# A two-layer diffusion backbone on one Trainium2 core: gated unit ahead of layer 1's first queries, block work between up and down, a reordered layer step

## The chip, the cores and the metric

The kernel runs on 1 core of one Trainium2 chip. Its time is the device time of one execution, in microseconds (us). The kernel before takes 1481.97 us, the median of 3 runs (1481.2 to 1482.17). One execution, taken with the hardware profiler, took 1484.51 us.

The core has five engines with a queue of instructions each: PE (TensorE, matrix products; PEld are its weight loads), DVE (VectorE), ACT (ScalarE), POOL (GpSimd) and SP (SyncE, which here only issues DMAs). 16 DMA engines carry data between HBM and the on-chip memory.

## The reference

256 latent tokens and 256 context tokens of width 1024 pass through two layers that share their weights between both streams. Everything is float32.

```python
for i in range(DEPTH):                                  # 2
    with_ctx_out = i < DEPTH - 1                        # layer 1: latents alone come out
    sh1, sc1, g1, sh2, sc2, g2 = split(silu(c) @ w_mod[i] + b_mod[i], 6)     # and csh1.. of c_ctx
    hl = modulate(rms_norm(x,  norm1_g[i]), sh1, sc1)
    hc = modulate(rms_norm(xc, norm1_g[i]), csh1, csc1)
    lat_mix, ctx_mix = token_mixers(hl, hc, ...)        # one projection w_in, three head groups:
        # A: global attention, 6 query heads on 2 key heads, q/k norm and rotary
        # B: gated unit u = a * sigmoid(g), depthwise convolution of 31 taps, layer norm, silu
        # C: window attention (+-128 tokens), 6 heads on 2, with a learned sink per head
    x = x + g1 * (lat_mix @ w_out[i])
    hl = modulate(rms_norm(x, norm2_g[i]), sh2, sc2)
    # the same for xc in layer 0
    y = hierarchical_moe(...)   # top 1 of 4 groups, top 2 of its 8 experts; 32 experts, each
                                # (silu(h @ w_gate[e]) * (h @ w_up[e])) @ w_down[e], 1024 -> 512 -> 1024
    x = x + g2 * y
return rms_norm(x, final_g)
```

## The kernel before, in words

Tokens lie in tiles of 128. Layer 0 works on four tiles (two latent, two context), layer 1 on two for all but keys and values. A float32 matrix product is split in a high and a low part (wh and wl of a weight, hH and hL of an activation), made by a cast on ACT and a difference on DVE or POOL, and taken as three products.

A layer runs in this order. **Modulation**: `mod_load` brings 4 MB of w_mod (tile wm) and returns `compute`, which makes 64 products `pm`. In layer 0 two groups of it stand at the start of the program; the others are put as fills between later products (list `todo`). **Norm and modulation of the tokens**: `rstd` and `modulate` give hT (high) and hL (low). **Projections**: `product_kv` (keys and values, pkv), `gated_unit` (pu), `first_queries` (A) and `project_q(1)` (C), whose steps for one k carry a number of convolution taps (`conv(cv[n][k])`) and of query and key steps (`st`); the tables `cv` and `st` of the configuration say how many. `query_tile` makes the tile tq, which PE then transposes (pqt). **Attention units**: S = q k, its maximum mx, P, its transposes pT, PT and po, for a pair of heads and a token tile; 12 units in layer 1. **Convolution's norm**, **output projection** (`load_wo`, pwo), **router**.

**Experts.** 32 experts go in 16 pairs, two pairs to a quad. `pair` makes gate and up (pgu: 16 products for each, weights in tile we, on half of the array, 64 columns), the product of silu and up (act), its transposes (pat), and down (py). A pair takes 12 weight loads of 1 MB from SP through a ring of eight slots. Four times in a pair `burst(i)` is called: after gate (0), after up (1), after the transposes (2), and in the middle of down (3). The list `at` says what stands in each: the gathers of the next quad's tokens (`mine`: a one-hot step, weights, gathers 0 to 7, written pg), and the eight `adders` of the pair before (two products pc and two DVE instructions each), which add its result to the tokens. pg, pat and pc use the array's whole width.

After layer 0's last pair, `finish` calls the last adders, squares the result (sq) and sums the squares over the tokens with products by ones (ss): layer 1's first norm.

What sets the order: engines PE, DVE and ACT are written out in order by `manual_schedule` in these stretches, SP throughout; else a scheduler places instructions. A record of the trace is not always one instruction: one float32 product appears as two.

Of the names in the rows, rope, gqk, rb, sinkb are small inputs (rotary table, norm gains, router bias, sinks); negsink is -sinkb, which C's softmax uses; wr are the router's weights.

## Time and profile before

| | |
|---|---|
| Time, median of 3 runs | 1481.97 us (1481.2 to 1482.17) |
| Profiled execution | 1484.51 us, of it the span 1482.9 us |
| PE busy | 1410.0 us, 95% |
| DVE busy | 612.1 us, 41% |
| ACT busy | 394.6 us, 27% |
| POOL busy | 85.9 us, 6% |
| DMA | 481.86 MB, mean 325 GB/s |

Layer 0's projections and attention lie before 300 us, its experts from about 313 to 803 us, layer 1's projections and attention to about 962, its router to 1006, its experts to the end. A share of busy time is a mean over stages with different limits; each stage is read for itself. The granted clock is 1.00 at 2.4 GHz and 0.50 at 1.2 GHz; a number between is a mean over a stretch with both.

### The profile page before, as it was taken

What the parts mean: (1) busy time and instruction counts of PE and PEld (TensorE: products, weight loads), DVE (VectorE), ACT (ScalarE), POOL (GpSimd) and SP (SyncE); (2) the same over time, 40 slices, a digit from 0 to 9 for tenths busy, and PEclk for the clock granted to TensorE, in tenths of its full rate; (3) what the DMA queues carried; (4) which work ended last, traced back from release to release, by engine and by line L of the source; (5) the groups of instructions that cost most, each with busy time, mean ns of one, the idle gap of its engine ahead of it and who ended that gap; (6) DMA issues with size and microseconds to landing.
All of it is one profiled execution on the core that took longest, in us unless ns stands there. A gap on an engine that the chain in (4) does not pass through costs nothing. (4 is left out here: it accounts for less than half of the span.)

```text
span 1482.9 us, 20526 instructions
## 1 busy us (share of the span) xinstructions
PE 1410.0 (95%) x8080; PEld 775.2 (52%) x8080; DVE 612.1 (41%) x1379; ACT 394.6 (27%) x954; POOL 85.9 (6%) x146
## 2 busy tenths in 40 slices
PE   6999899999999999998999998989999999999997
PEld 4777677754444544444435776774443343333432
DVE  3469884353223333333334568853222222222223
ACT  3454575430111111100102555652111111110102
POOL 3212000100000000000001020010000000000000
PEclk8999999999999999999999899999999999999999
DMA  9847502399799999999999583087999999999996
GB/s 312 315 156 260 138 2 103 153 359 371 319 402 411 415 409 407 417 408 397 390 401 383 203 292 89 4 361 290 371 419 422 420 421 422 421 420 421 420 418 257
DMA packets 92324, 481.86 MB, mean 325 GB/s; under 512 B 8884, under 2 KB 17296, under 8 KB 47040
## 3 DMA queue, kind: packets, MB, share of 16 engines
q1 hardware_dynamic: 90960, 478.19, 81.3%
q0 software_dynamic: 800, 1.20, 0.4%
q8 instruction: 66, 1.08, 0.3%
q10 hardware_dynamic: 464, 1.11, 0.2%
q14 instruction: 34, 0.28, 0.0%
HBM read 479.42 MB, written 1.05 MB: 324 GB/s over the span
## 5 line engine op out<-in xcount | busy, mean ns | idle before, releaser
L1340 PE MATMUL pgu<-we,xg 128*64 128x512 f32 x1904 | 450.8, 598 | 23.4 <-DMA we<-in_w_gate_dram 13.1
L1340 PEld LDWEIGHTS pgu<-we,xg 128*64 128x64 f32 x1904 | 143.5, 137 | 308.8 <-issue 251.6
L1394 PE MATMUL py<-we,actT 128*64 128x512 f32 x888 | 205.8, 597 | 0.7 <-ACT actT L1355 0.7
L1236 DVE SCALAR_TENSOR_TENSOR xT<-pc,mod,xT 128x256 f32<-128x256 f32 x256 | 104.8, 476 | 177.4 <-PE pc L1233 177.4
L1394 PEld LDWEIGHTS py<-we,actT 128*64 128x64 f32 x888 | 61.9, 136 | 114.8 <-issue 110.8
L1290 ACT COPY xg<-pg 128x256 f32<-128x256 f32 x112 | 36.3, 376 | 309.8 <-PE pg L1286 309.8
L1349 DVE SCALAR_TENSOR_TENSOR act<-pgu,ws,sil 128x512 f32<-128x512 f32 x32 | 24.0, 751 | 194.0 <-PE pgu L1340 185.1
L1244 DVE TENSOR_TENSOR xo<-xo,pc 128x512 f32<-128x512 f32 x62 | 39.8, 683 | 111.3 <-PE pc L1243 111.3
L1285 PE MATMUL pg<-OH,hH 128*128 128x256 f32 x336 | 84.2, 290 | 0.0
L1286 PE MATMUL pg<-OH,hL 128*128 128x256 f32 x336 | 81.7, 283 | 0.0
L634 DVE SCALAR_TENSOR_TENSOR ca<-gpad,cw,ca 128x512 f32<-128x512 f32 (+1 forms) x120 | 73.3, 611 | 0.9
L1285 PEld LDWEIGHTS pg<-OH,hH 128*128 128x128 f32 x336 | 64.2, 191 | 11.4 <-issue 10.5
L281 PE MATMUL pm<-wm,scT 128*32 128x256 f32 (+1 forms) x896 | 64.3, 370 | 2.2 <-DMA wm<-in_w_mod_dram 2.0
L1286 PEld LDWEIGHTS pg<-OH,hL 128*128 128x128 f32 x336 | 64.3, 191 | 0.0
L1344 ACT ACTIVATE sil<-pgu 128x512 f32<-128x512 f32 x32 | 19.2, 598 | 167.1 <-PE pgu L1340 167.1
L1259 DVE TENSOR_TENSOR Yg<-py,g2r 128x512 f32<-128x512 f32 x31 | 21.3, 688 | 100.8 <-PE py L1394 96.5
L1363 POOL CAST se<-ident 32x128 fp32r<-32x128 f32 x32 | 9.1, 286 | 900.8 <-PE pb L1364 871.0
L1261 ACT CAST YH<-py 128x512 fp32r<-128x512 f32 x32 | 18.7, 586 | 151.3 <-PE py L1394 134.4
L1261 ACT CAST YH<-Yg 128x512 fp32r<-128x512 f32 x31 | 19.1, 618 | 141.2 <-DVE Yg L1259 141.2
L1232 PE MATMUL pc<-oht,YH 128*128 128x512 f32 x128 | 55.2, 432 | 0.2 <-ACT YH L1261 0.2
L1233 PE MATMUL pc<-oht,YL 128*128 128x512 f32 x128 | 50.6, 395 | 0.2 <-DVE YL L1262 0.2
L1262 DVE TENSOR_TENSOR YL<-py,YH 128x512 fp32r<-128x512 f32 x32 | 22.1, 691 | 61.2 <-ACT YH L1261 61.2
(434 smaller groups left out, 2125.4 us busy)
## 6 DMA issues: line engine op xcount, KB each, us to landing
we<-in_w_up_dram SPq DMA_DIRECT2D x112, 1024.0 KB, 8.9
we<-in_w_down_dram SPq DMA_DIRECT2D x111, 1024.0 KB, 11.2
we<-in_w_gate_dram SPq DMA_DIRECT2D x110, 1024.0 KB, 11.8
wm<-in_w_mod_dram SPq DMA_DIRECT2D x44, 1024.0 KB, 11.0
wp<-in_w_gate_dram SPq DMA_DIRECT2D x8, 1024.0 KB, 11.2
wp<-in_w_up_dram SPq DMA_DIRECT2D x8, 1024.0 KB, 10.3
we<-in_w_gate_dram SPq DMA_DIRECT2D x16, 512.0 KB, 11.0
we<-in_w_up_dram SPq DMA_DIRECT2D x16, 512.0 KB, 10.2
```

The source lines that it names most:

```text
L281: pe.matmul(p[0][32 * q:32 * q + 32], scT[:, kq, :], ws[128 * kq // nr][:, kq % (nr // 128), c:c + n], start=k == 0, stop=k == KC * nq // ...
L634: ve.scalar_tensor_tensor(a, g, wt, a, op0=OP.mult, op1=OP.add)
L1232: pe.matmul(pc, YH[:, 128 * o:128 * o + 128], oht, start=True, stop=False)
L1233: pe.matmul(pc, YL[:, 128 * o:128 * o + 128], oht, start=False, stop=True)
L1236: ve.scalar_tensor_tensor(xT[:, o, sl], pc[:, sl], mod[l][:, 5, o, s:s + 1], xT[:, o, sl], op0=OP.mult, op1=OP.add)
L1244: ve.tensor_tensor(xo[t][:, sl], xo[t][:, sl], pc, op=OP.add)
L1261: sc.copy(YH[:rows, sl], py)
L1285: pe.matmul(dst, hH[t][:, 128 * k:128 * k + 128], rhs, start=t == 0, stop=False)
L1286: pe.matmul(dst, hL[t][:, 128 * k:128 * k + 128], rhs, start=False, stop=t == NT - 1)
L1290: sc.copy(xg[e][:, k - 1:k + 1, :], v[:, :, e])
L1340: pe.matmul(p[64 * e:64 * e + 64, m, :], xg[:, k, 64 * e:64 * e + 64], w_[e](k % 4), start=k == 0, stop=k == KC - 1)
L1394: pe.matmul(py[64 * e:64 * e + 64, h], actT[:, 128 * f + 64 * e:128 * f + 64 * e + 64], wd[e](f % 2)[:, 512 * h:512 * h + 512], start=f == ...
```

## The change

Six edits, told by place.

1. *Start of the program.* The rotary table and ten small broadcast loads go from POOL's queue, ahead of the weights, to SP's queue (`small_inputs`), behind the first four groups of weights. The router's weights wr go from POOL's queue at the start of a layer to SP's, just ahead of `load_wo`. Of the dummy products of PE, 20 behind the first modulation group become 4, and 12 stand behind the second.
2. *Between the layers.* `compute` is cut in `products` and the rest, so that `finish` can place parts of layer 1's modulation group (m = 2) between the sums; the squares are added up on POOL and DVE to three tiles rather than five; eight dummies and the casts of the key and value weights stand ahead.
3. *Layer 1.* The gated unit comes ahead of the first queries; taps are 2 per k in `first_queries` and 3 per k in `project_q(1)`, before 4 per k in the latter alone.
4. *Attention units* take two consecutive heads (2j and 2j + 1), before heads j and 3 + j; `load_wo` so loads 128 rows at a time, before pieces of 64.
5. *Pairs of layer 0 that gather for a next quad* (13 of 16): nothing but the one-hot step stands between gate and up, nothing in the middle of down; all else stands between up and down, ahead of and behind the transposes.
6. SP issues layer 1's weights in the order in which they are now used.

```diff
@@ -191,23 +191,23 @@
     rope_t = per.tile([128, 2, 2, 64], F32, name="rope")
-    gp.dma_start(rope_t, rope)
-    def bcast_load(t, src, n):
-        gp.dma_start(t, bass.AP(tensor=src.tensor, offset=src.offset, ap=[[0, 128], [1, n]]))
     gqk = per.tile([128, DEPTH, 2, 64], F32, name="gqk")
...
     sinkb = per.tile([128, DEPTH, 6], F32, name="sinkb")
-    for l in range(DEPTH):
-        bcast_load(gqk[:, l, 0, :], qg_d[l], 64)
-        bcast_load(gqk[:, l, 1, :], kg_d[l], 64)
-        bcast_load(rb[:, l, 0:4], bgrp_d[l], 4)
-        bcast_load(rb[:, l, 4:36], bexp_d[l], 32)
-        bcast_load(sinkb[:, l, :], sink_d[l], 6)
     negsink = per.tile([128, DEPTH, 3, 2], F32, name="negsink")
-    gp.tensor_scalar(negsink, sinkb.rearrange("p l (h j) -> p l j h", h=2), -1.0, None, op0=OP.mult)
+    def bcast_load(t, src, n, eng=gp):
+        eng.dma_start(t, bass.AP(tensor=src.tensor, offset=src.offset, ap=[[0, 128], [1, n]]))
+    def small_inputs():
+        sp.dma_start(rope_t, rope)
+        for l in range(DEPTH):
+            bcast_load(gqk[:, l, 0, :], qg_d[l], 64, sp)
+            bcast_load(gqk[:, l, 1, :], kg_d[l], 64, sp)
+            bcast_load(rb[:, l, 0:4], bgrp_d[l], 4, sp)
+            bcast_load(rb[:, l, 4:36], bexp_d[l], 32, sp)
+            bcast_load(sinkb[:, l, :], sink_d[l], 6, sp)
+        gp.tensor_scalar(negsink, sinkb.rearrange("p l (j h) -> p l j h", h=2), -1.0, None, op0=OP.mult)
@@ -270,16 +270,20 @@
-        def compute(two=False, eng=gp, between=None, p=None):
+        def products(ks=range(KC * nq // 4), two=False, p=None):
             if p is None:
...
                 p = p[:, 0:n], p[:, n:n + 16]
-            for k in range(KC * nq // 4):
+            for k in ks:
                 for q in range(4):
...
                               start=k == 0, stop=k == KC * nq // 4 - 1)
+            return p
+        def compute(two=False, eng=gp, between=None, p=None, made=None):
+            p = made or products(two=two, p=p)
             s = K2("ms", (128, n), tag="m")
...
@@ -462,15 +467,9 @@
-        r1 = rstd(ssq0 if l == 0 else ss1[0], 4, D, "n1")
-        if l > 0:
-            finish_mods(l, 1)
         w = win_d[l]
...
         gp.memset(wr[:, :, 36:], 0.0)
-        gp.dma_start(wr[:, :, 0:4], wgrp_d[l].rearrange("(k p) g -> p k g", p=128))
-        gp.dma_start(wr[:, :, 4:36], wexp_d[l].rearrange("(k p) g -> p k g", p=128))
-        h_mul, h_scale, h_shift, hH, hL = modulate(l, r1)
@@ -492,16 +491,19 @@
         first = []
-        if l > 0:
-            early = mod_load(*todo.pop(0), 0, 8)
         for j in range(4):
...
                 load_u(j)
+        if l == 0:
+            small_inputs()
         wKV = lambda k: wkv[k // 4][:, k % 4, :]
         wU = lambda k: wu[k // 2][:, k % 2, :]
+        if l > 0:
+            ws = Splits(wKV, 512)
+        h_mul, h_scale, h_shift, hH, hL = modulate(l, rstd(ss1[0] if l else ssq0, 4, D, "n1"))
@@ -534,12 +536,15 @@
         if l > 0:
+            early[0].products(range(5, 8), p=early[1])
+            pw_ = P1("warm")
+            for _ in range(8):
+                pe.matmul(pw_[:, 0:256], identb, masks.rearrange("p a b -> p (a b)"), start=True, stop=True)
             h_mul(0)
             h_scale(0)
-            ws = Splits(wKV, 512)
             trans.close()
             with tc.high_priority(offset=-cfg["fpri"]):
-                early(True)
+                early[0](made=early[1])
         dve_order = ExitStack()
@@ -550,7 +555,9 @@
         cf = cfg["fill"][l]
-        cv = cfg["cv"][l]
+        cv = cfg["cv"][0] if l == 0 else ((0,) * KC, (2,) * KC, (3,) * KC)
+        st = cfg["st"][0] if l == 0 else ((0, 1, 0, 1, 0, 0, 1, 0), (0, 1, 0, 0, 1, 0, 0, 0), (0, 1, 0, 1, 1, 0, 0, 0))
@@ -578,12 +585,16 @@
+            def dummies(n):
+                for _ in range(n):
+                    pe.matmul(pm[:, 1, 256:512], identb, masks.rearrange("p a b -> p (a b)"), start=True, stop=True)
             modulation(0)
             mul_to(3)
-            for _ in range(20):
-                pe.matmul(pm[:, 1, 256:512], identb, masks.rearrange("p a b -> p (a b)"), start=True, stop=True)
+            dummies(4)
             modulation(1)
+            dummies(12)
             splits(0)
...
@@ -760,7 +771,7 @@
         todo_steps += [key_rstd] + [lambda i=i: key_tile(i, phase[0] == 2) for i in range(4)]
-        for f in (gated_unit, first_queries) if cfg["u1"][l] else (first_queries, gated_unit):
+        for f in (gated_unit, first_queries):
             f()
@@ -799,15 +810,16 @@
             nb = 1 if i < 2 else 2
...
                 for h in range(2):
-                    q = qT[g](3 * h + j, 128 * (i + b))
+                    q, kv = qT[g](2 * j + h, 128 * (i + b)), (2 * j + h) // 3
                     masked = g == 1 and i < 2
                     o, ks = (S[:, h, :], slice(0, 512)) if i < 2 else (S[:, h, 256 * b:256 * b + 256], slice(256, 512))
-                    pe.matmul(o, q, kH[g][:, h, ks], start=True, stop=False)
-                    pe.matmul(o, q, kL[g][:, h, ks], start=False, stop=not masked)
+                    pe.matmul(o, q, kH[g][:, kv, ks], start=True, stop=False)
+                    pe.matmul(o, q, kL[g][:, kv, ks], start=False, stop=not masked)
                     if masked:
...
@@ -923,12 +936,13 @@
             t = [slot("wo").rearrange("p (c f) -> p c f", f=1024) for _ in range(4)]
-            for n, part in enumerate((((0, 0, 2),), ((0, 128, 1), (1, 640, 1)), ((0, 704, 2),))):
-                for h in range(2):
-                    for i, r, m in part:
-                        r += 192 * h
-                        sp.dma_start(t[n][64 * h:64 * h + 64, i:i + m, :], src[r:r + 64 * m].rearrange("(j d) f -> d j f", d=64))
-            sp.dma_start(t[3], src[384:640].rearrange("(c p) f -> p c f", p=128))
+            for n in range(4):
+                c0, c1 = order[2 * n:2 * n + 2]
+                if c1 == c0 + 1:
+                    sp.dma_start(t[n], src[128 * c0:128 * c0 + 256].rearrange("(c p) f -> p c f", p=128))
+                else:
+                    for i, c in enumerate((c0, c1)):
+                        sp.dma_start(t[n][:, i], src[128 * c:128 * c + 128])
             at = {c: (i // 2, i % 2) for i, c in enumerate(order)}
@@ -963,6 +977,8 @@
+        sp.dma_start(wr[:, :, 0:4], wgrp_d[l].rearrange("(k p) g -> p k g", p=128))
+        sp.dma_start(wr[:, :, 4:36], wexp_d[l].rearrange("(k p) g -> p k g", p=128))
         wo = load_wo()
@@ -1537,13 +1553,20 @@
                     q = sq_[o] = square(o, N)
-                    if o in (1, 2, 3):
+                    if o in (1, 2, 3, 4):
                         gp.tensor_tensor(sq_[0], sq_[0], q, op=OP.add)
+                    if o == 6:
+                        ve.tensor_tensor(q, sq_[5], q, op=OP.add)
                 if h == 1:
+                    f = mod_load(*todo.pop(0), 0, 8)
+                    made = f.products(range(2), two=True)
                     p = P1("ss1")
-                    for i, o in enumerate((0, 4, 5, 6, 7)):
-                        sum_tokens(p, sq_[o], NT, i == 0, i == 4)
+                    for i, o in enumerate((0, 7, 6)):
+                        sum_tokens(p, sq_[o], NT, i == 0, i == 2)
+                    f.products(range(2, 5), p=made)
                     ss1.append(p[:, :NT])
+                    early.extend((f, made))
                 return
@@ -1587,10 +1610,18 @@
                     hot = 1 if len(mine) > 4 else 0
-                    at = [adders[:3] + mine[:hot] if qd or e else [weights], mine[hot:6], adders[3:5], adders[5:]]
-                    at[3] += mine[6:]
-                    if not mine:
-                        at[1], at[2] = at[2], []
+                    if mine and not last:
+                        g = mine[hot:]
+                        head, g = (g[:1], g[1:]) if hot else ([], g)
+                        a_ = adders
+                        at = [mine[:hot], head + a_[:2] + g[:2] + a_[2:4],
+                              a_[4:5] + g[2:4] + a_[5:6] + g[4:6] + a_[6:7] + g[6:] + a_[7:], []]
+                    else:
+                        at = [adders[:3] + mine[:hot] if qd or e else [weights], mine[hot:6], adders[3:5], adders[5:]]
+                        at[3] += mine[6:]
+                        if not mine:
+                            at[1], at[2] = at[2], []
                     if qd == 0 and e == 0:
```

On PE, at the end of layer 0's last pair: the last adder (pc), the sums (ss), modulation (pm), the norm's broadcast (rb) and layer 1's first key and value products (pkv). Before:

```order
L1233 MATMUL pc<-oht,YL 128x512
L418 MATMUL ss_6622<-ones,sq 128x1 x4
L281 MATMUL pm<-wm,scT 32x256 x8
L418 MATMUL ss_6622<-ones,sq 128x1 x12
L281 MATMUL pm<-wm,scT 32x256 x3
L418 MATMUL ss_6622<-ones,sq 128x1 x4
L281 MATMUL pm<-wm,scT 32x256 x13
L339 MATMUL rb<-ident,n1r 128x128 x4
L291 MATMUL pm<-ident,ms 128x8 x2
L558 MATMUL pkv<-wh,hT 128x512 x4
```

Now (the pair of weight load and dummy `warm` stands eight times):

```order
L1249 MATMUL pc<-oht,YL 128x512
L281 MATMUL pm<-wm,scT 32x256 x8
L423 MATMUL ss_6633<-ones,sq 128x1 x12
L281 MATMUL pm<-wm,scT 32x256 x12
L344 MATMUL rb<-ident,n1r 128x128 x4
L281 MATMUL pm<-wm,scT 32x256 x12
L542 LDWEIGHTS identb
L542 MATMUL warm<-masks,identb 128x256
...
L565 MATMUL pkv<-wh,hT 128x512 x2
L295 MATMUL pm<-ident,ms 128x8 x2
```

All pm of this group now stand behind the adders, twelve of them behind the broadcast, and the sums are one run of 12 rather than 20 in three runs.

On PE, in a pair of layer 0's experts that gathers, from the transposes (pat) through down (py) to the next pair's gate (pgu); pb is a broadcast that the gather needs. Before:

```order
L1353 MATMUL pat<-ident,act 128x128 x4
L1232 MATMUL pc<-oht,YH 128x512
L1233 MATMUL pc<-oht,YL 128x512
L1232 MATMUL pc<-oht,YH 128x512
...
L1364 MATMUL pb<-posT,se 128x512
L1394 MATMUL py<-we,actT 64x512 x8
L1232 MATMUL pc<-oht,YH 128x512
L1233 MATMUL pc<-oht,YL 128x512
...
L1394 MATMUL py<-we,actT 64x512 x8
L1340 MATMUL pgu<-we,xg 64x512 x16
L1232 MATMUL pc<-oht,YH 128x512
```

Now, from the last gather on:

```order
L1248 MATMUL pc<-oht,YH 128x512
L1249 MATMUL pc<-oht,YL 128x512
L1380 MATMUL pb<-posT,se 128x512
L1410 MATMUL py<-we,actT 64x512 x16
L1356 MATMUL pgu<-we,xg 64x512 x32
L1248 MATMUL pc<-oht,YH 128x512
L1249 MATMUL pc<-oht,YL 128x512
```

The adders inside down are gone to the stretch ahead of it, and so are those behind gate: the next pgu is gate and up in one run.

On DVE, in layer 1, around the first query tiles (tq, of A's queries) and the convolution's taps (ca). Before, tq stand ahead of the first tap:

```order
L438 TENSOR_TENSOR t_7452<-qn,rope 128x12x16 x2
L722 TENSOR_TENSOR tq<-qn,tq 128x4x64
L722 TENSOR_TENSOR tq<-qn,tq 128x2x64
L439 TENSOR_TENSOR qn<-t_7451,t_7452 128x384
L722 TENSOR_TENSOR tq<-qn,tq 128x4x64
L722 TENSOR_TENSOR tq<-qn,tq 128x2x64
L517 TENSOR_TENSOR gpad<-pu,sg 128x256
L632 TENSOR_SCALAR ca<-gpad,cw,vb 128x256
L634 SCALAR_TENSOR_TENSOR ca<-gpad,cw,ca 128x256 x2
```

Now 46 taps stand ahead of the same tq:

```order
L438 TENSOR_TENSOR t_7633<-qn,rope 128x384
L443 TENSOR_TENSOR t_7634<-qn,rope 128x12x16 x2
L645 SCALAR_TENSOR_TENSOR ca<-gpad,cw,ca 128x256
L387 TENSOR_TENSOR wl<-wo,wh 128x512
L733 TENSOR_TENSOR tq<-qn,tq 128x4x64
L733 TENSOR_TENSOR tq<-qn,tq 128x2x64
L645 SCALAR_TENSOR_TENSOR ca<-gpad,cw,ca 128x256
L444 TENSOR_TENSOR qn<-t_7633,t_7634 128x384
```

The taps have moved ahead of A's queries, and the softmax maxima (mx) behind them.

## Rows read from the trace of the kernel before

**Rows 1.** Stretches: us; PE, PEld, DVE, ACT, POOL busy; clock; DMA share; GB/s

```profile
9.00:13.50 4.50, 1.93 (x13) 1.72 (x13) 1.57 (x3) 3.08 (x5) 3.02 (x6) 0.84 0.95 185
31.40:35.80 4.40, 4.21 (x11) 3.06 (x12) 1.02 (x2) 0.85 (x2) 0.34 (x1) 0.63 1.05 387
40.00:60.00 20.00, 19.98 (x198) 15.68 (x197) 10.03 (x23) 7.70 (x18) 2.95 (x4) 1.00 1.05 391
437.40:498.50 61.10, 61.10 (x310) 28.69 (x308) 20.21 (x44) 7.11 (x16) 0.57 (x2) 1.00 1.00 412
810.80:827.80 17.00, 14.95 (x70) 10.78 (x70) 7.42 (x20) 6.06 (x15) 0.33 (x1) 0.50 1.04 369
828.00:885.00 57.00, 56.54 (x404) 43.76 (x402) 35.27 (x83) 30.20 (x77) 10.11 (x11) 1.00 0.60 213
909.80:916.60 6.80, 5.26 (x21) 3.93 (x21) 6.28 (x17) 4.59 (x14) 0.00 (x0) 0.50 0.01 2
925.00:955.00 30.00, 30.00 (x267) 22.66 (x266) 26.00 (x79) 18.91 (x58) 0.00 (x0) 1.00 0.01 1
1080.00:1450.00 370.00, 349.81 (x1566) 140.72 (x1562) 83.95 (x144) 43.48 (x94) 3.75 (x12) 1.00 1.01 420
```

**Rows 2.** DMA queues and issues of 0 to 60 us

```profile
q0 software_dynamic: 576, 0.52, 7.4%
...
wU<-in_w_in_dram SPq DMA_DIRECT2D x4, 512.0 KB, 10.7
```

**Rows 3.** Timeline of PE: start, us, engine, line, instruction

```profile
21.95 4.01 PE L585 MATMUL pm<-masks,identb 128*128 128x256 bf16 x20 [0.26 <-DVE mod L298]
...
31.39 0.50 PE L558 MATMUL pkv<-wh,hT 128*128 128x512 f32 x1 [1.85 <-ACT hT L365]
```

**Rows 4.** Timeline of ACT, 28 to 34 us

```profile
30.52 0.40 ACT L526 CAST wu<-wU 128x256 fp32r<-128x256 f32 x1 [0.76 <-DMA wU<-in_w_in_dram]
```

**Rows 5.** Timeline of PE in a pair of layer 0

```profile
459.70 3.65 PE L1394 MATMUL py<-we,actT 128*64 128x512 f32 x16
463.29 0.50 PE L1232 MATMUL pc<-oht,YH 128*128 128x512 f32 x1
463.62 0.39 PE L1233 MATMUL pc<-oht,YL 128*128 128x512 f32 x1
...
464.55 0.40 PE L1233 MATMUL pc<-oht,YL 128*128 128x512 f32 x1
464.88 3.65 PE L1394 MATMUL py<-we,actT 128*64 128x512 f32 x16
468.36 1.03 PE L1340 MATMUL pgu<-we,xg 128*64 128x512 f32 x4
```

**Rows 6.** Timeline of PE between the layers

```profile
806.99 0.39 PE L1233 MATMUL pc<-oht,YL 128*128 128x512 f32 x1
...
808.10 1.07 PE L281 MATMUL pm<-wm,scT 128*32 128x256 f32 x16
809.10 3.78 PE L418 MATMUL ss<-ones,sq 128*128 128x1 f32 x24
...
822.98 1.65 PE L558 MATMUL pkv<-wh,hT 128*128 128x512 f32 x3 [2.05 <-ACT wh L380]
```

**Rows 7.** What PE waited for, 800 to 1010 us: us, times, longest

```profile
PE pqt L725 <- DVE tq L722: 3.3, 1, 3.3
...
PE cr L339 <- DVE cn2r L333: 2.0, 1, 2.0
PE pT L843 <- ACT P L829: 1.4, 1, 1.4
```

**Rows 8.** Tile ca, 823 to 960: ns min/median/max, first and last start

```profile
L634 DVE SCALAR_TENSOR_TENSOR ca<-gpad,cw,ca x60: 464/477/486, 886.0 to 959.4; 128x256 f32<-128x256 f32 x60
```

**Rows 9.** Timeline of POOL, 30 to 60 us

```profile
54.23 0.74 POOL L527 TENSOR_TENSOR wu<-wU,wu 128x256 fp32r<-128x256 f32 x1 [5.70 <-ACT wu L526]
```

**Rows 10.** Timeline of SP's queue, 30 to 60 us

```profile
39.73 1.84 SPq L91 DMA_DIRECT2D wU<-in_w_in_dram  x1
```

14 lines of the change are left out of this document (8 added, 6 removed).

## The prediction

> **What bounds the kernel now.** I read the busy time, clock and DMA rate by stretch first [rows 1]. The reader is to see three kinds of stretch. In layer 0's experts (437.4 to 498.5 us is one quad, that is two pairs) TensorE is busy 61.10 of 61.10 us at full clock while the DMA engines show a share of 1.00 at 412 GB/s: PE sets the end, but the loads are hardly behind. In layer 1's experts (1080 to 1450) PE is busy only 349.8 of 370 us and the rate lies flat at 420 GB/s: there the loads set the end, and the change edits nothing in that stretch, so whatever starts it earlier is passed on whole. Between them lie thin stretches in which PE waits or runs at half clock: 31.4 to 35.8 (granted 0.63), 810.8 to 827.8 (0.50), 909.8 to 916.6 (0.50). Then I read the timelines of boot and boundary [rows 2 to 4, 6, 9, 10], of one expert pair [rows 5], and what PE waits for in layer 1 [rows 7], with DVE's taps [rows 8]. So the change can act in four places, and I price each from its own rows.
>
> **Boot (small loads from POOL's queue to SP, behind the first weights; fewer dummies, later).** The software queue's packets took 7.4% of 16 engines over 60 us [rows 2], which is 4.4 us. While they run, 9 to 13.5 us, the rate is 185 GB/s; at 40 to 60 us it is 391 [rows 1]. The shortfall is 4.5 x 206 GB/s = 0.93 MB, or 2.4 us at 391. The first projection waits 1.85 us for hT [rows 3], which stands on ACT behind a cast that waited for a weight wU [rows 4]: a chain fed by the DMA queue, so I let it come 2.4 us sooner. The first matmuls run at 0.63, of 4.4 us that is 1.6 us lost; the 12 dummies that now stand directly ahead may give it back. They cost 12 x 0.2 us (20 took 4.01 [rows 3]) = 2.4, against the 1.85 us of idle time they fill; that 4 and not 20 stand ahead of the second modulation group I don't count. Ends: 4.4 + 1.6 = 6.0 at best, and -0.6 (the dummies alone, all else hidden). I take 3, near the 2.4 that the rates give plus part of the clock.
>
> The Trainium skill (DMA: Bandwidth & Descriptors, "Issuing engines are not separate DMA queues") says that transfers of all issuing engines end up on the same 16 DMA engines and interleave. That speaks against this part: moved to another queue, the same packets cost the same, only later. By it the gain would be what lies before the first projection, and 4.4 us come back if the later queue has no room; the 40 to 60 stretch, with PE and DMA both full, bears that out as a risk, and the sum by it would be about 1 us for boot instead of 3.
>
> One wait is added: POOL's negsink waits for the last small load. It stands behind 4 splits of wU and ahead of 12 that the gated unit's products use. Before, the fifth split ran at 54.23 [rows 9]. SP issues the small loads behind the last weight of the first stage (at 39.73, lasting 1.84 [rows 10]); with the 10.7 us from issue to landing of these weights [rows 2] I estimate their landing at 50 to 52. It is free until about 53 us (54.23 less some 1 us for negsink itself and an earlier boot); each us later stalls POOL and, through the splits, PE.
>
> **Layer 0's experts (block work gathered between up and down).** Rows of one pair [rows 5]: in the run of six full-array adder matmuls between half-array py, starts lie 0.23 us apart inside (463.62 to 464.55 is four steps), but 0.33 at entry and 0.33 at exit; and 16 py take 3.59 us with the switch behind them (459.70 to 463.29), 3.48 without one. So a run costs 0.10 + 0.10 + 0.11 = 0.3 us beyond its matmuls. Before, a pair has three runs (between gate and up, around the transposes, inside down); after, one. Two runs x 0.3 x 13 pairs that are changed = 7.8 us of PE. But DMA is the floor: a quad moves 61.1 us x 412 GB/s = 25.2 MB, which at layer 1's 420 GB/s takes 59.9 us, exactly PE's 61.1 - 4 x 0.3. With both engines at the same number small jitter costs; I take 70%: 5.5 us, ends 0 and 7.8. The gathers' and adders' own matmuls are only moved; ACT and DVE (7.1 and 20.2 us of 61.1) have room for the denser burst. The up weights are now needed right behind gate, some 1.6 us sooner: that is the rival below.
>
> On that floor the Trainium skill (DMA: Bandwidth & Descriptors, "Specifications") gives about 358 GB/s from HBM per core and 435 as the fabric's ceiling. By 358 a quad would need 70 us, the loads would bind already and this part would give nothing; the rows show 412 and 420 on this lone core, so the measurement decides. By 435 a quad would take 57.9 us and the whole 7.8 would come.
>
> **The boundary to layer 1.** From the last adder's start (806.99) to the first projection (822.98) PE takes 16.0 us [rows 6]: norm sums (40 records; 24 of them take 3.78 us), modulation matmuls, broadcast, 2.05 us idle for the weight cast wh. After, sums are 24 records rather than 40 (16 x 0.157 = 2.5 us less), two of three adds going to POOL and DVE; all modulation matmuls now stand behind the adders (16 records more: 16 took 1.07 us), half of them behind the broadcast, in what was idle; the weight cast stands ahead of hT on ACT; eight dummies (1.6 us) fill the rest. I get 2.5 - 1.1 + 2.05 = 3.4 us sooner, and from 823 to 827.8 the half clock costs 2.4 us, of which I give the dummies half: 4.6, rounded to 4.5. Ends: 0.7 (a third of the idle time, because the chain of squares, root and scaling sets the time) and 7 (2.5 + 2.05 + 2.4).
>
> **Layer 1's attention (gated unit ahead of the first queries, taps spread over both query projections).** PE's waits there [rows 7]: 3.3 us for the query tile tq, behind taps on DVE; 1.4 for a softmax P; 2.0 for the convolution's norm. The half clock at 909.8 follows the first and costs 2.6 us (half of PE's 5.26). Together 9.3 us. The norm's 2.0 goes almost surely: taps, which end at 959.4 now [rows 8], come earlier. The other two are less sure: after, 46 of 62 taps (0.477 us each: 21.9 us) stand ahead of the first query tile, and before the first scores DVE has 57 - 35.3 = 21.7 us free (828 to 885 [rows 1]). That just balances, so I take 5, ends 0 and 9.3. In the units themselves (925 to 955) PE is busy 30.00 of 30, so DVE's relief there is worth nothing. Consecutive heads pair up in a unit with the same matmul count.
>
> **At nothing:** w_out loaded over 128 partitions and the router's weights on SP's queue; both are loaded under the attention, where SP has nothing else to fetch (2 GB/s at 909.8 to 916.6, 1 at 925 to 955 [rows 1]); without that cover w_out's 4 MB would take 10 us at 420.
>
> **Sum.** 3 + 5.5 + 4.5 + 5 = 18 us. The profiled execution took 1484.51 us (span 1482.9), 2.5 above the median of 1481.97; so 1466.5 in its own terms, 1464 as a median.
>
> **Rivals.**
> A. One term fails. The loads bind in layer 0's experts already (DMA share 1.00): 1469.5. Or DVE, with 21.9 us of taps before the queries, hands the attention's idle time back: 1469. Or PE stays too thin at the boundary to regain its clock and the norm chain sets it: 1468. Or POOL stands at negsink, worth its 3 us and up to 4 more: 1467 to 1471. For it speaks that each has a row showing the second engine nearly as full; against, that they are independent. Two together: 1472 to 1476.
> B. Everything works: 6 + 7.8 + 7 + 9.3 = 30: 1452. Speaks against it the DMA floor.
> C. Slower: up's weights. With gate and up contiguous, up is due 1.6 us earlier in each of 13 pairs, and slots of the ring come free in other places. If PE waits w us per pair for them, the experts change by 13 x (w - 0.6); at w = 2 that is +18 against the other parts' -12.5: 1488. It decides from w = 1.6. For it: loads run at share 1.00; against: PE waits for none of them now (61.10 of 61.10), and DMA that loses time in one pair has 1.2 us per quad to regain it.
> D. The change does not do what it says: places are rearranged and the waits reappear next door, all within 3 us of 1482.
>
> **Chances.** Forecast (1458 to 1470, where a single failed term lies as well): 0.58. Two terms fail (1470 to 1479): 0.18. B, below 1458: 0.08. D: 0.07. C, above 1485: 0.09. I call the range 1453 to 1479. Two parts in a thousand, 3 us, is about what a measurement can tell from no change: faster 0.84, same 0.07, slower 0.09.
>
> **What would show it.** In the changed profile: pairs of layer 0's experts about 0.4 to 0.6 us shorter each, PE still without gaps and the rate near 420; no "py, adders, py" rows. The first pkv about 2 to 3 us sooner, at full clock early. Fewer than 16 us from last adder to layer 1's first pkv, and a shorter half-clock stretch than 17 us. The waits for tq and cn2r gone, no new wait of over 2 us for a query tile. The last stretch of unchanged length. I am wrong if PE waits for up's weights in the pairs, or if layer 1's attention shows as much idle time as before.

## The result, and the profile after

The changed kernel takes 1476.07 us (median of 6 runs, 1475.14 to 1479.22) where the kernel before took 1483.69 in the same comparison (6 runs, 1481.2 to 1486.4). The ratio is 0.9948, with a 95% interval of 0.9932 to 0.9965: about 7.7 us faster (5 to 10). The forecast was 18 us faster.

The profiled execution took 1475.36 us, its span 1473.4, so 9.5 us less than the span of before. PE's timeline gives the points between which it went (us; a minus is a gain). The table compares one execution with one; how far each stretch varies stands at the head of the experiments.

| From, to | before | after | change | forecast |
|---|---|---|---|---|
| start to layer 0's last key product | 71.4 | 64.3 | -7.2 | -3 |
| to its first scores | 77.5 | 77.4 | -0.1 | 0 |
| to its first expert | 164.7 | 162.6 | -2.1 | 0 |
| to its last adder | 493.4 | 493.3 | -0.1 | -5.5 |
| to layer 1's last key product | 40.3 | 36.0 | -4.4 | -4.5 (with the clock) |
| to its first expert | 159.0 | 163.6 | +4.6 | -5 |
| to the end | 476.6 | 476.2 | -0.3 | 0 |

The stretches of the changed kernel that answer to [rows 1], in the same columns (start and end; length; PE, PEld, DVE, ACT, POOL busy; clock; DMA share; GB/s):

```profile
9.00:13.50 4.50, 3.68 (x50) 2.84 (x49) 1.61 (x4) 4.21 (x7) 0.00 (x0) 1.00 1.06 385
26.40:31.00 4.60, 4.60 (x21) 3.59 (x19) 1.34 (x3) 1.24 (x4) 0.74 (x1) 0.97 1.05 387
40.00:50.00 10.00, 10.00 (x101) 7.99 (x100) 5.07 (x11) 3.95 (x9) 0.73 (x1) 1.00 0.42 128
426.07:487.71 61.64, 60.07 (x309) 29.13 (x307) 20.02 (x44) 7.31 (x16) 0.57 (x2) 1.00 1.00 409
801.50:808.30 6.80, 6.18 (x40) 4.48 (x40) 2.12 (x7) 2.33 (x5) 0.00 (x0) 0.50 1.07 374
850.60:887.50 36.90, 34.11 (x290) 24.81 (x289) 33.44 (x77) 20.03 (x50) 9.55 (x10) 1.00 0.89 319
887.50:907.30 19.80, 10.56 (x36) 7.21 (x34) 18.46 (x45) 7.62 (x19) 1.58 (x1) 0.57 0.05 19
907.30:953.00 45.70, 44.97 (x423) 34.84 (x422) 31.44 (x81) 30.49 (x93) 0.00 (x0) 1.00 0.01 1
1071.00:1441.00 370.00, 350.33 (x1565) 142.19 (x1562) 83.99 (x144) 43.50 (x95) 3.75 (x12) 1.00 1.01 421
```

What is to be seen: the dip of the loads at 9 to 13.5 us is gone (385 GB/s, before 185), and the first projection runs at nearly full clock. The dip now lies at 40 to 50 us (128 GB/s), where PE is busy 10.00 of 10.00 us all the same. A quad of layer 0's experts takes 61.64 us, longer than before's 61.10, and PE is no longer busy throughout. Between the layers the half clock lasts 6.8 us, before 17.0. But in layer 1 DVE is now busy 33.4 of 36.9 and 18.5 of 19.8 us, and PE only 10.6 of these 19.8. Layer 1's experts are as before.

The new wait in the experts, PE's timeline of one pair (start, length, instruction, in brackets the idle time ahead and what ended it), and ACT's beside it:

```profile
457.33 7.04 PE L1356 MATMUL pgu<-we,xg 128*64 128x512 f32 x32
465.15 7.09 PE L1356 MATMUL pgu<-we,xg 128*64 128x512 f32 x32 [0.78 <-ACT sil L1360]
...
480.79 7.09 PE L1410 MATMUL py<-we,actT 128*64 128x512 f32 x32
487.71 1.88 PE L1356 MATMUL pgu<-we,xg 128*64 128x512 f32 x7
```

```profile
464.50 0.60 ACT L1360 ACTIVATE sil<-pgu 128x512 f32<-128x512 f32 x1 [5.00 <-PE pgu L1356]
```

Up's first product waits until ACT's silu of gate has ended (464.50 + 0.60). Before, six adder matmuls, 1.6 us long, stood in that place and hid it. The runs of adders themselves were saved as forecast: all 16 py of a pair (32 records) now go without a break, where [rows 5] shows them cut in two.

What PE waits for from 790 to 1000 us (total, times, longest), to be held against [rows 7]:

```profile
PE pqt L736 <- DVE tq L733: 4.4, 2, 2.5
PE pT L855 <- ACT P L841: 3.9, 2, 3.6
...
PE pq L678 <- DVE wl L387: 2.2, 2, 1.1
PE ss L423 <- ACT sq L417: 1.4, 1, 1.4
...
PE cr L344 <- DVE cn2r L338: 0.8, 1, 0.8
...
PE ss L423 <- POOL sq L1557: 0.7, 1, 0.7
```

The wait for the query tile is not gone but 4.4 us in two, the one for P has grown from 1.4 to 3.9, and two waits for DVE's weight splits wl are new. Only the convolution's norm gave up time (2.0 to 0.8).

### The profile page after: what moved, and what is told of

Same layout as the page of the kernel before. It is cut to its first block, busy times and chain, and to the rows that moved or that the text cites. A ratio compares the mean times of both kernels' runs of the same rounds, so it can differ in the third digit from the quotient of the medians.

```text
span 1473.4 us, 20487 instructions
## 1 busy us (share of the span) xinstructions
PE 1389.8 (94%) x8068; PEld 771.9 (52%) x8068; DVE 617.2 (42%) x1380; ACT 396.8 (27%) x955; POOL 81.2 (6%) x132
## 5 line engine op out<-in xcount | busy, mean ns | idle before, releaser
L1356 PE MATMUL pgu<-we,xg 128*64 128x512 f32 x1904 | 449.2, 598 | 31.6 <-DMA we<-in_w_gate_dram 12.8
L1252 DVE SCALAR_TENSOR_TENSOR xT<-pc,mod,xT 128x256 f32<-128x256 f32 x256 | 104.8, 477 | 53.0 <-PE pc L1249 52.1
L281 PE MATMUL pm<-wm,scT 128*32 128x256 f32 (+1 forms) x896 | 59.8, 359 | 3.2 <-DMA wm<-in_w_mod_dram 3.1
## 6 DMA issues: line engine op xcount, KB each, us to landing
we<-in_w_gate_dram SPq DMA_DIRECT2D x110, 1024.0 KB, 13.5
wp<-in_w_up_dram SPq DMA_DIRECT2D x8, 1024.0 KB, 10.6
```

Of the source, the lines that this page charges most:

```text
L281: pe.matmul(p[0][32 * q:32 * q + 32], scT[:, kq, :], ws[128 * kq // nr][:, kq % (nr // 128), c:c + n], start=k == 0, stop=k == KC * nq // ...
L1252: ve.scalar_tensor_tensor(xT[:, o, sl], pc[:, sl], mod[l][:, 5, o, s:s + 1], xT[:, o, sl], op0=OP.mult, op1=OP.add)
L1356: pe.matmul(p[64 * e:64 * e + 64, m, :], xg[:, k, 64 * e:64 * e + 64], w_[e](k % 4), start=k == 0, stop=k == KC - 1)
```

## The experiments

Stages are compared between profiled executions; a whole time has its ratio to the kernel before, run beside it on the same chip. The runs also show how far a stretch varies where its code is the same, so that a whole time says less than a stage, and a stage is held against these ranges (us):

| Stretch | code of the changed kernel | code of before |
|---|---|---|
| start to layer 0's last key product | 64.3 to 66.1 (11 executions) | 71.4 (1) |
| layer 0's first scores to the last part of its units | 94.6 to 96.8 (8) | 97.2, 98.8 |
| first gate to last down in layer 0 | 488.2 to 489.3 (7) | 489.1 to 491.1 (4) |
| last adder to layer 1's last key product | 34.7 to 37.4 (8) | 40.3, 36.9, 36.7 |
| from there to layer 1's first expert | 163.6 to 165.0 (6) | 158.3 to 159.8 (4) |

**Own PSUM tiles for gate and up.**

```diff
-            p = P2("pgu")
+            p = [P2("pgu")[:, 0], P2("pgu")[:, 0]]
...
-   pe.matmul(p[64 * e:64 * e + 64, m, :], xg[:, k, ...
+   pe.matmul(p[m][64 * e:64 * e + 64, :], xg[:, k, ...
```

> The changed kernel, but gate and up of a pair of experts write two PSUM tiles of their own, where both write halves of one. In the changed kernel PE waits 0.78 us per pair between gate and up for ACT's silu of gate. Theory (the wait hangs on the shared tile, and the adders that used to stand there hid it): the wait is gone, pairs of layer 0 take 30.4 and 29.5 us rather than 31.27 and 30.37, layer 0's experts (489.3 us from the first gate to the last down) about 10 us less, the whole 1466. Rival (the loads are the floor): the wait moves to the loads, the quad stays at 61 or more, gain under 3 us. Rival (the silu is needed for another reason): the wait stays at 0.78.

Measured: 1467.82 us, ratio 0.9895 (0.9878 to 0.9913). From the first gate to the last down 478.5 us, 10.8 less than the changed kernel; the whole is only 8 us faster, since in the profiled execution the start and layer 1's attention, whose code is the same, took 1.6 and 1.4 us longer. PE's timeline, and two quads in the columns above:

```profile
456.76 14.09 PE L1356 MATMUL pgu<-we,xg 128*64 128x512 f32 x62
...
479.41 7.09 PE L1410 MATMUL py<-we,actT 128*64 128x512 f32 x32
486.33 3.17 PE L1356 MATMUL pgu<-we,xg 128*64 128x512 f32 x14
```

```profile
456.30:517.00 60.70, 60.70 (x309) 30.28 (x307) 20.02 (x44) 7.31 (x16) 0.57 (x2) 1.00 1.01 415
517.00:577.60 60.60, 60.60 (x309) 29.55 (x307) 20.02 (x44) 7.31 (x16) 0.57 (x2) 1.00 1.01 417
```

Gate and up are one run without a gap: the wait hung on the shared tile, not on the work. The fastest pairs of either kind take 30.26 and 29.37 us, 1.0 less than the changed kernel's 31.27 and 30.37, so a wait of 0.78 costs 1.0 with what it breaks up. But most pairs of the first kind take 30.7 to 31.2, and the quad falls by 1.0 us, not by 2.0. At 415 to 417 GB/s and a share of 1.01 it lies close to the 59.9 us that the loads were worked out to take, and PE's weight loads from 400 to 640 us now show a wait (total, times, longest) that the changed kernel has nowhere in that stretch:

```profile
PEld pgu L1356 <- DMA we<-in_w_up_dram: 2.4, 6, 0.8
```

One of the six, in the pair from 425.62, on PEld's timeline:

```profile
436.32 0.19 PEld L1356 LDWEIGHTS pgu<-we,xg 128*64 128x64 f32 x3 [0.27 <-DMA we<-in_w_up_dram]
```

By the trace this load of up's weights lands at 436.28, and the weight load behind it was due at 435.92 with the one before it: PE is 0.4 us late. So the loads take part of the gain back: what rival C feared, up's weights coming late, shows once the wait for silu is gone.

**Block work as before**, all else changed.

```diff
-                    if mine and not last:
+                    if False:
```

> The changed kernel with the block work of a pair put back as before (adders between gate and up and inside down). Theory (two runs fewer save 0.5 us per pair, the bare wait for the silu costs 0.8): pairs return to 31.00 and 30.11, that is 0.27 us shorter each, layer 0's experts 2 to 4 us shorter. What the prediction said: 0.4 to 0.6 us longer per pair, 5.5 us in all.

Measured: 1479.27 us, ratio 0.9968 (0.9952 to 0.9983). Pairs take 31.00 and 30.11 us again, 0.27 less than the changed kernel's, as expected. But from first gate to last down it is 489.5 us against 489.3: no gain of 2 to 4. What the steady pairs lose in the changed kernel, the second and third pair (2.3 us from second to fourth gate, 68.56 to 66.31) and those around the branch for overfull experts (65.92 to 64.41) give back. So the edit was worth little in sum, about 1 us by the ranges above, where 5.5 was forecast. The whole is 3 us above the changed kernel's; in the profiled executions that lies at the start, between the layers and in layer 1 (1.0, 1.3 and 0.6 us), where the code is the same.

**24 taps ahead of the first query tile.**

```diff
-        cv = cfg["cv"][0] if l == 0 else ((0,) * KC, (2,) * KC, (3,) * KC)
+        cv = cfg["cv"][0] if l == 0 else ((0,) * KC, (2,) * KC, (2,) * KC)
...
                     unit(g, j, i)
+                    conv(3)
...
```

(3 taps are written behind each unit, the rest ahead of the norm, where all that were left stood ahead of the units.)

> The changed kernel, with 24 taps of layer 1's convolution ahead of the first query tile on DVE where it has 46: 2 taps per k in both query projections, 3 per attention unit. Theory (taps ahead delay the query tile): about 22 x 0.43 = 9 us of DVE work less ahead of it, the first scores come 5 to 9 us earlier, after the first key product, than the changed kernel's 83.6 us; idle time and half clock of 887 to 907 us shrink, the experts of layer 1 start 4 to 8 us earlier. Rival (the gated unit, which covered the chain of the queries' norm, is gone from its place): the first scores come within 2 us of now.

Measured: 1471.8 us, ratio 0.9919 (0.989 to 0.9949, 2 runs, 6.4 us apart). In the trace 22 taps stand ahead of the first query tile. First scores 76.9 us after the first key product (changed kernel 83.6, before 62.8); last key product to first expert 157.3 us rather than 163.6. The stretch that was at 0.57 of the clock:

```profile
887.80:900.00 12.20, 8.11 (x50) 5.86 (x49) 11.98 (x29) 6.42 (x16) 1.05 (x1) 0.86 0.07 26
```

The half clock lasts 3.4 us there (894.8 to 898.2), not 17.1. The taps ahead were the cost: with 24 of them the stretch takes 157.3 to 160.3 us in three executions (the last two versions below are the others), about what the old order takes.

**w_out in pieces of 64 rows**, heads paired as before.

```diff
-                    sp.dma_start(t[n], src[128 * c0:128 * c0 + 256].rearrange("(c p) f -> p c f", p=128))
...
+                        sp.dma_start(t[n][64 * h:64 * h + 64, i:i + m, :], src[r:r + 64 * m].rearrange("(j d) f -> d j f", d=64))
...
```

> The changed kernel with the pairing of heads and the loads of w_out as before (64 rows at a time). Theory (in layer 0 ACT stands at a cast of w_out until the load lands, and the softmax behind it is late): PE's wait for P near 153 us goes from 1.6 back to about 4 us, layer 0's attention takes 2.1 us longer from the first scores to the last, all else the same. Rival (the heads' pairing changes the units themselves): units are longer throughout, without that one wait.

Measured: 1481.35 us, ratio 0.9978 (0.9966 to 0.999). From layer 0's first scores to the last part of its units 99.1 us, the changed kernel 95.0, before 97.2. ACT's timeline before, changed, and in this run:

```profile
158.66 1.14 ACT L380 CAST wh<-wo 128x512 fp32r<-128x512 f32 x2 [3.77 <-DMA wo<-in_w_out_dram]
```

```profile
149.82 1.14 ACT L385 CAST wh<-wo 128x512 fp32r<-128x512 f32 x2 [1.68 <-DMA wo<-in_w_out_dram]
```

```profile
152.58 1.14 ACT L385 CAST wh<-wo 128x512 fp32r<-128x512 f32 x2 [3.31 <-DMA wo<-in_w_out_dram]
```

And PE behind it, before, changed, and in this run:

```profile
161.69 1.78 PE L843 MATMUL pT<-ident,P 128*128 128x128 f32 x8 [4.12 <-ACT P L829]
```

```profile
153.37 1.32 PE L855 MATMUL pT<-ident,P 128*128 128x128 f32 x8 [1.61 <-ACT P L841]
```

```profile
157.70 1.12 PE L854 MATMUL pT<-ident,P 128*128 128x128 f32 x4 [4.78 <-ACT P L840]
```

On ACT the casts of w_out stand ahead of a softmax, and until the load lands the softmax waits, and PE behind it. The stretches in which w_out lands show why (the columns of [rows 1]): before and in this run, in pieces of 64 rows, and changed, 128 rows at a time.

```profile
156.40:163.10 6.70, 2.57 (x26) 2.02 (x21) 4.35 (x10) 4.44 (x14) 1.27 (x1) 0.94 1.03 230
150.10:161.90 11.80, 7.02 (x46) 5.28 (x45) 8.20 (x14) 6.76 (x22) 1.26 (x1) 0.83 1.03 224
149.80:154.90 5.10, 3.48 (x34) 2.81 (x35) 5.10 (x9) 5.08 (x17) 1.44 (x1) 1.00 1.02 414
```

With the DMA engines as busy in each (share 1.02 to 1.03), pieces of 64 rows come at 230 and 224 GB/s, 128 rows at 414. The heads' pairing, which goes back with the loads, was not tried apart, but the wait for P takes 3.2 of the 4.0 us. The wait is longer here than before (4.8 to 4.1): the router's weights now stand ahead of w_out on SP's queue, as the run with the small loads alone, below, shows more plainly.

**Layer 1's projections in the order of before.**

```diff
-        cv = cfg["cv"][0] if l == 0 else ((0,) * KC, (2,) * KC, (3,) * KC)
...
+        cv = cfg["cv"][0] if l == 0 else cfg["cv"][1]
...
-        for f in (gated_unit, first_queries):
+        for f in (gated_unit, first_queries) if l == 0 else (first_queries, gated_unit):
```

(The table `st` of the query and key steps goes back as well.)

> The changed kernel with layer 1's projections in the order of before: first queries, then the gated unit, 4 taps per k in the second query projection alone. Theory (the reorder of layer 1 costs 4.6 us from the last key product to the first expert, and it is the taps and the lost cover that cost it): that stretch returns from 163.6 to about 159 us, the whole 4 to 5 us faster than the changed kernel. What the prediction said: 5 us slower than the changed kernel.

Measured: 1472.05 us, ratio 0.9913 (0.9884 to 0.9942, 2 runs). Last key product to first expert 159.8 us; first scores 61.0 us after the first key product. As the theory had it, the reorder with its 46 taps was a loss of about 4 us, not a gain of 5. Order and taps go back together here, so this run alone does not say which of them cost it; the run with 24 taps does: the taps.

**No tap ahead of the first query tile.**

```diff
-        cv = cfg["cv"][0] if l == 0 else ((0,) * KC, (2,) * KC, (3,) * KC)
+        cv = cfg["cv"][0] if l == 0 else ((0,) * KC, (0,) * KC, (0,) * KC)
```

> The changed kernel with no tap written into the projections of layer 1: 0 of 62 taps stand ahead of the first query tile (46 in the changed kernel, 24 in the one with fewer). Theory (a line in the taps ahead, 0.3 us each as measured between 46 and 24): first scores 70 us after the first key product (83.6 and 76.9 with 46 and 24), but 62 taps then stand in the units, which DVE's free time of some 14 us there can't hold: the units take over 3.9 us each and the stretch to the experts is no shorter than with 24 taps. Rival (the first scores wait for the lost cover of the gated unit): they come at 75 us or later.

Measured: 1477.97 us, ratio 0.9963 (0.9944 to 0.9982). First scores at 77.3 us, no earlier than with 24 taps: the line of the theory is wrong below 24, and the rival's number right. The taps then fill the units, in columns as above:

```profile
900.00:957.00 57.00, 48.37 (x432) 37.26 (x430) 52.05 (x144) 33.23 (x99) 0.00 (x0) 0.94 0.00 1
```

DVE is busy 52.1 of 57.0 us, PE 48.4, and last key product to first expert takes 164.4 us. The rival's reason, the lost cover of the gated unit, does not hold. From the first key product to the first scores, before, changed, and with 24 taps:

```profile
822.98:885.82 62.84, 62.03 (x419) 48.19 (x419) 40.78 (x96) 34.46 (x87) 10.11 (x11) 0.96 0.64 231
811.16:894.76 83.60, 75.63 (x542) 58.40 (x539) 68.45 (x158) 42.69 (x103) 17.61 (x18) 0.97 0.65 231
811.06:888.00 76.94, 74.86 (x542) 58.47 (x540) 58.39 (x131) 42.48 (x105) 14.84 (x18) 1.00 0.70 251
```

In the old order half of the query products (48 of 96 records) and a third of the modulation stand behind the first scores; in the new order, with 46 or 24 taps, all of them stand ahead. So nearly all of the way from 62.8 to 77 us is PE's own work, only moved (12.8 us more busy time), and no loss. The loss is in the idle time: 0.8 us before, 8.0 with 46 taps, 2.1 with 24.

**The small loads alone**, in the kernel before.

```diff
...
+        if l == 0:
+            small_inputs()
...
+        sp.dma_start(wr[:, :, 0:4], wgrp_d[l].rearrange("(k p) g -> p k g", p=128))
+        sp.dma_start(wr[:, :, 4:36], wexp_d[l].rearrange("(k p) g -> p k g", p=128))
         wo = load_wo()
```

> The kernel before with one edit: the small loads go from POOL's queue to SP's behind the first weights, the router's weights to SP ahead of w_out; dummies, order and all else as before. Theory (these loads are what holds up the start): first key product 3 to 5 us earlier than 31.39, last key product 4 to 6 earlier than 71.41. Rival (the dummies give it): under 1.5 us earlier. A second expectation: with 64-row loads of w_out behind the router's weights, the wait for P near 157 us is no shorter than the 4.1 us of before.

Measured: 1481.11 us, ratio 0.9985 (0.9969 to 1.0002, not told from no change as a whole). First key product at 25.70 us (before 31.39), last at 65.89 (71.41): 5.5 us. Then the wait for P takes 3 back:

```profile
158.90 0.90 PE L843 MATMUL pT<-ident,P 128*128 128x128 f32 x3 [6.88 <-ACT P L829]
```

6.9 us rather than 4.1. SP's queue shows the router's weights ahead of w_out:

```profile
137.86 5.00 SPq L967 DMA_DIRECT2D wr<-in_w_expert_dram  x1
```

So the first load of w_out is issued 0.4 us ahead of layer 0's first scores, before 3.3 us.

**The dummies alone**, in the kernel before.

```diff
-            for _ in range(20):
+            for _ in range(4):
...
             modulation(1)
+            for _ in range(12):
...
```

> The kernel before with one edit: 4 dummies behind the first modulation group and 12 behind the second, where 20 stood behind the first. Theory (they hold the clock up for the first key products, nothing else): first key product within 1 us of 31.39, matmuls 0.23 us apart from there on rather than 0.43 until 35.7, so the last key product 1 to 2 us earlier than 71.41. Rival (they give most of the 7 us): 4 us or more earlier.

Measured: 1485.2 us, ratio 1.0009 (0.9995 to 1.0023, not told from no change as a whole). First key product at 31.72, last at 70.13: 1.3 us, by the clock alone. 5.5 and 1.3 make 6.8; executions of the changed start show 5.3 to 7.2.

This run shows something else, for the code between the layers is that of before here. From the last adder to the last key product it takes 36.9 us, not 40.3; the small loads alone take 36.7. PE's timeline of this run, to be held against [rows 6]:

```profile
809.52 2.84 PE L418 MATMUL ss<-ones,sq 128*128 128x1 f32 x24
820.67 2.00 PE L558 MATMUL pkv<-wh,hT 128*128 128x512 f32 x4 [2.22 <-ACT wh L380]
```

The granted clock is at 0.50 for 6.8 us in all here (814.0 to 817.4 and 820.8 to 824.2), as long as in the changed kernel; in the profiled execution of before it was 17.0 us. So most of the table's 4.4 us at the boundary came with that execution and not with the change.

**The dummies between the layers left out.**

```diff
-            for _ in range(8):
+            for _ in range(0):
```

> The changed kernel without the eight dummies ahead of layer 1's first key product. Theory (the clock is full again 2 us before the dummies begin, at 808.3, so they only fill a wait for hT): from the last adder to the first key product 13.0 to 13.6 us as now (13.55), and from there to the last key product 22.4 as now. What the prediction said: they give back half of 2.4 us of half clock, so 1.2 us longer without them.

Measured: 1476.56 us, ratio 0.9947 (0.9926 to 0.9968). Last adder to first key product 13.1 us (13.55 with them), from there to the last 22.4 as with them. They give nothing: 0.4 us is less than what executions of the same code differ by.

**Five sums rather than three.**

```diff
...
-                    for i, o in enumerate((0, 7, 6)):
+                    for i, o in enumerate((0, 4, 5, 6, 7)):
```

> The changed kernel with the squares of layer 0's end summed from five tiles rather than three (40 records of PE rather than 24, one addition less each on POOL and DVE). Theory (fewer sums on PE shorten the way to layer 1's first norm): from the last adder to the first key product 1.5 to 2.5 us longer than the 13.55 of now. Rival (the chain of squares on ACT and additions on POOL and DVE sets it: PE waits 0.7 and 1.4 us there): no longer, or shorter.

Measured: 1477.97 us, ratio 0.9962 (0.9943 to 0.998). Last adder to first key product 11.74 us, 1.8 less than the changed kernel's 13.55. Eight executions with three sums take 12.2 to 15.0, so the size is rough, but both with five (the other is the last one below) lie under all of them. PE's timeline in the changed kernel and here:

```profile
797.61 0.39 PE L1249 MATMUL pc<-oht,YL 128*128 128x512 f32 x1
797.93 1.07 PE L281 MATMUL pm<-wm,scT 128*32 128x256 f32 x16
799.68 1.05 PE L423 MATMUL ss<-ones,sq 128*128 128x1 f32 x8 [0.68 <-POOL sq L1557]
802.12 3.58 PE L423 MATMUL ss<-ones,sq 128*128 128x1 f32 x16 [1.39 <-ACT sq L417]
...
811.16 0.71 PE L565 MATMUL pkv<-wh,hT 128*128 128x512 f32 x2
```

```profile
801.16 0.40 PE L1249 MATMUL pc<-oht,YL 128*128 128x512 f32 x1
801.49 1.07 PE L281 MATMUL pm<-wm,scT 128*32 128x256 f32 x16
802.49 4.63 PE L423 MATMUL ss<-ones,sq 128*128 128x1 f32 x40
```

40 records in one run without a wait take 4.6 us; 24 with the additions ahead take 6.0 (799.68 to 805.63), 1.4 of it idle, behind 0.7 us more of idle time. Part of the rest is half clock: the 16 records of 3.58 us take 2.05 in the run with the old projection order. DVE's timeline in the changed kernel says why: its addition, which waits 0.76 us for a square, stands ahead of the last adder's two instructions, so the last square on ACT, which PE waits for, comes late.

```profile
799.87 0.69 DVE L1559 TENSOR_TENSOR sq<-sq 128x512 f32<-128x512 f32 x1 [0.76 <-ACT sq L417]
800.48 0.87 DVE L1252 SCALAR_TENSOR_TENSOR xT<-pc,mod,xT 128x256 f32<-128x256 f32 x2
```

The rival was right.

**The findings together**: own tiles, 24 taps ahead, the router's weights behind w_out.

> A version built from the findings: the changed kernel with PSUM tiles of their own for gate and up, 24 taps of layer 1 ahead of the first query tile rather than 46, and the router's weights issued behind w_out rather than ahead of it. If the three act in places of their own, the gains over the changed kernel add up: 10.8 us in layer 0's experts, 6.3 in layer 1's attention, and up to 1.6 in layer 0's attention (the wait for P that is left near 153 us): 1476 - 18.7 = about 1457. Rival (layer 0's experts gain 10.8 only because the loads had been fetched ahead elsewhere; the loads take the rest back): 1462 or more.

Measured: 1460.59 us, ratio 0.9834 (0.9818 to 0.985). Layer 0's first scores to last part of a unit 93.8 us (changed 95.0), experts 477.8 (489.3), last key product to first expert 160.3 (163.6). That is 3 us more than with 24 taps alone; the half clock lasts 17.1 us in that stretch, there 6.8. The sum of the three parts, 1457, is missed by 3.6 us, 3 of them here; the rival's 1462 is not reached, and the experts hold their gain. What the place of the router's weights is worth is not shown: 93.8 lies 1 us under the range above, and the version below has 94.8, within it.

**The same with five sums and no dummies between the layers.**

> The version of the combined findings once more, with two further changes: the squares of layer 0's end summed from five tiles as before, and no dummies ahead of layer 1's first key product. By the two runs that did one of these alone (1.8 and 0.45 us less from the last adder to the first key product) that way is 11.3 to 11.8 us rather than 13.55, and the whole about 2 us below the combined version's 1460.6, if the clock is no lower for it; rival: without dummies and with more thin sums the half clock lasts into the key products and takes it back.

Measured: 1455.08 us (5 runs, 1454.5 to 1457.45), ratio 0.9809 (0.9792 to 0.9825); against the changed kernel that is 0.9809 / 0.9948 = 0.986. Last adder to first key product 11.3 us, half clock there 3.4 us. The gain over the version above is 5.5 us where 2 was expected: 2.3 lie between the layers, and 2.9 in layer 1's attention (157.4 us, half clock 6.8 us rather than 17.1), whose code is the same. This version beats both kernels.

## Why the prediction was right or wrong

The direction was right, the size was not: 7.7 us for 18. The time lies in the range, where rival A had "Two together: 1472 to 1476" and the chances gave that case 0.18. Two terms did fail, but in ways the rivals name only in part.

**Layer 0's experts: the step that failed is "Two runs x 0.3 x 13 pairs that are changed = 7.8 us of PE", with ACT put at nothing because "ACT and DVE (7.1 and 20.2 us of 61.1) have room".** The price of a run was near, rather low: the fastest pair with own tiles takes 29.37 us for before's 30.11, that is 0.74 for two runs. What was missing is what the removed work had covered, silu: 1.0 us a pair, so that a pair became 0.27 longer. A busy share of 7.1 of 61.1 us says nothing of when silu ends. The text even said that gate and up come together, and asked only whether up's weights would be late (rival C). In the changed kernel they were not; with own tiles they are, by 0.4 us in a pair such as the one named above. The wait could have been read: in `pair`, silu reads one half of the tile p whose other half up writes, and a silu of 0.6 us cannot end before up would start. The guess of rival A, that the loads bind already, is not what took the gain, since own tiles gave 10.8 us. On the loads' floor the prediction weighed the Trainium skill (DMA: Bandwidth & Descriptors, "Specifications"): some 358 GB/s per core from HBM. The quads with own tiles ran at 415 and 417, so here too the measurement decides; it is nearer to the 435 that the Trainium skill gives there for the fabric.

**Layer 1's attention: the step that failed is "That just balances, so I take 5".** It set 21.9 us of taps against DVE's free time from 828 to 885 us. But a tap needs the gated unit's result, and free time ahead of that can't be used. In the changed kernel the first tap runs at 854.1, and the first query tile is written at 889.9; from the first key product to the first tap, and from there to the query tile:

```profile
811.16:854.10 42.94, 42.94 (x263) 34.33 (x261) 29.30 (x69) 23.91 (x56) 6.48 (x8) 1.00 0.55 200
854.10:889.90 35.80, 30.92 (x270) 22.64 (x268) 34.29 (x78) 17.26 (x43) 11.13 (x10) 1.00 0.85 300
```

DVE is idle for 13.6 us where no tap can run yet, and busy 34.3 of 35.8 us where they do. PE's waits follow, and the half clock with them: 2.6 us of its cost were to be saved, and it now costs 5.1 (half of PE's 10.26 us busy from 890.2 to 907.3). From the last key product to the first expert PE is idle 17.8 us, before 12.6, which was one of the prediction's own signs of being wrong. Rival A had the mechanism with DVE as the bound, but at a loss of 0, not 4.6 beyond it. With 24 taps PE is idle 12.8 us in that stretch, as before: the reorder itself then costs nothing and saves no idle time either, so the runs show no 5 to be had from it.

**"At nothing: w_out loaded over 128 partitions"** failed too, to the good: 2.1 us between the two profiled executions, 4 by the run that undoes it. The text looked at layer 1, where SP's queue is empty, and named no layer 0, where ACT's casts wait for exactly this load. The same sentence passed the router's weights, which stand ahead of it and cost up to 3 us of that when w_out is in small pieces.

**Boot** was right in its mechanism and too small: 5.5 us for the loads, 1.3 for the dummies' clock, where 3 was taken between -0.6 and 6.0. The mis-sized term is the 2.4 us of missing rate: besides the rate, a wait of PE for b_mod's load went that the prediction has no row of, and the clock did not fall at 12.1. PE before:

```profile
12.64 0.47 PE L226 MATMUL pv<-ident,vec 128*128 128x128 f32 x1 [2.48 <-DMA vec<-in_b_mod_dram]
```

The wait that was added did no harm: negsink ran on POOL inside the 50 to 52 us expected, after 8.5 us of standing, and PE waited for nothing behind it.

```profile
50.09 0.25 POOL L210 TENSOR_SCALAR negsink<-sinkb 128x12 f32<-128x12 f32 x1 [8.47 <-DMA sinkb<-in_sink_dram]
```

The prediction weighed a rule of the Trainium skill against this part (DMA: Bandwidth & Descriptors, "Issuing engines are not separate DMA queues"): all queues end on the same DMA engines. The trace agrees in that the dip did not vanish: from 40 to 50 us the rate is 128 GB/s, before 384. But PE is busy 10.00 of 10.00 us there, and the 5.5 us are whole up to layer 0's first scores: the loads went to a place where PE did not wait for them.

**The boundary** came out at 4.4 us for 4.5 between the two profiled executions, and that is luck. Against the two other executions of the old code, 36.9 and 36.7 us, the gain is 1.0 and 0.7; what it is on average the runs don't settle. Nor do the terms hold: three sums for five cost some 1.8 us where 2.5 was credited, because PE waits for the additions. The sums had also been priced at 0.157 us each from a stretch half of which ran at half clock; in one run at full clock 40 take 4.63, 0.12 each. The dummies gave nothing where 1.2 was credited. Only the wait of 2.05 us for the weight cast went as forecast: it is not among PE's waits in the changed kernel.

## What to carry to other kernels

Before work is moved out of a gap, list every instruction that waited, covered, in that gap, on all engines, and the shared tiles that tie the neighbours; a wait that shows nowhere in the profile of before is not one that isn't there. Free time of an engine counts only from when the data for the moved work exist to when the result is needed. A cast of loaded data on an engine's queue makes the load's landing part of whatever stands behind it there. And a point such as the first scores compares two orders only if the same work stands ahead of it in both; a stretch is known only from more than one execution of the same code.

## What the runs showed of the hardware

Two PE products into different halves of one PSUM tile were ordered by a wait on the reader of the other half: 0.78 us in each pair, gone when each product has a tile of its own. Whether the chip needs such a wait, or only the program's order by tile makes it, these runs don't show. Loads of w_out over 64 partitions came at 224 and 230 GB/s, over 128 at 414, with the DMA share at 1.02 to 1.03 in each; the time from issue to landing does not show it as well (8 to 13 us and 6 to 12 over the runs). And the granted clock fell to 0.50 at the end of PE's wait of 2.5 us for the query tile and stayed there for 17.1 us (890.2 to 907.3) through the waits that followed, where with 24 taps it was 3.4 us: a wait on PE can cost more than its own length. It does not do so each time: between the layers the same code ran with 17.0 us of half clock in one execution and with 6.8 in two others, 3.4 and 3.7 us faster.
